# Third and fourth chain of an output projection's first pair change places; four small steps come later

## The chip, the cores and the metric

The kernel runs on one core of a Trainium2 chip. The metric is the device time of one execution in microseconds; 2374.19 is the median of the runs of the kernel before. Engines are named as in the profile: PE is TensorE's matmuls, PEld its weight loads, DVE is VectorE, ACT is ScalarE, POOL is GpSimd, SP is SyncE, whose queue starts the weight transfers.

## The reference

Two residual layers over 256 positions of width 2048 in float32, each followed by a SwiGLU feed-forward block; RMSNorm ahead of every part and once at the end.

```
for layer in range(2):
    h = rms_norm(x, mix_norm[layer])
    if layer == 0:   # Mamba-2 SSD heads and latent-attention (MLA) heads behind one input projection
        z, xbc, dt_raw, c_q, c_kv, k_rope = split(h @ w_in)
        y_ssd = ssd_mixer(z, xbc, dt_raw, ...)       # dt = softplus(dt_raw + dt_bias); decay = exp(cumsum(dt * a))
        y_mla = mla_mixer(c_q, c_kv, k_rope, ...)    # 16 heads, softmax, k_pe = rope(k_rope)
        mix = concat(y_ssd, y_mla) @ w_out_even      # 4096 x 2048
    else:            # stick-breaking attention: log_keep = -softplus(z), cumulative sums, exp
        mix = stick_breaking_mixer(h, w_qkv, w_out_odd)
    x = x + mix
    x = x + (silu(n @ w_gate) * (n @ w_up)) @ w_down   # n = rms_norm(x, ffn_norm[layer])
return rms_norm(x, final_norm)
```

## The kernel before, in words

**Words.** Every float32 product is done in three passes: an operand is parted into high words (a cast on ACT, L345) and low words (source minus high words on DVE, L351), and high x high, low x high and high x low are added up in PSUM. A weight tile is 512 rows by 512 columns. It comes by DMA into a slot `w`; its high words go into one of the slots `wh` (three, later four, in turn), its low words overwrite the raw tile in its own slot. The casts of the weights keep the order of the chains in which they are used, whose order on PE is fixed.

**Pairs.** `pair` multiplies an operand by a pair of column blocks in the manner of Strassen and Winograd: seven products of sums, M1 to M7, go into four PSUM banks. M1, M6 and M7 add into bank z, M5 and M3 into p3, M2 into p2, M4 into p4. The rest of the depth is done in plain chains c0 to c3. In this text a chain is one such product on PE: 8 matmuls with a tile's high words and then 4 with its low words (all L786). After M1, M5, M6 and M7 ACT copies the bank out of PSUM (L807); the next chain on that bank waits for the copy.

**Sums of weights.** Two slots `wsum` hold sums that DVE makes (L733): t1 = b12 - b11 is the source of M5, t2 = b22 - t1 that of M6, b12 becomes b22 - b12, the source of M7, and M4's source is b21 - t2. As there are two slots, M4's source is written into the slot of M5's, after the last product that reads it there; it reads t2, so it must be done before M6's low words overwrite t2.

**Order.** PE runs in the order in which the program is written. ACT, DVE, POOL and SP are ordered by a scheduler after priorities: `urgent` gives steps that free a bank an early one, weights have a count that rises by 100 a step (`wprio`), and `issue_after` puts a step behind another. Small steps run as tasks beside the chains: `yield n` lets a task rest for n ticks, and a chain gives two ticks (one after half its high words), a projection's group of 12 matmuls in the plain parts about two.

**Where the changed lines work.** `project_residual` runs two pairs; the first uses the order LATE, the second HALF. It runs three times: for the SSD heads at about 320 us, for the MLA heads at about 512 us and for stick-breaking at about 1585 us. `norm_operand` and `operand_block` take a finished residual block apart again: 4 transposes for each half of the positions (L356), products with the gains (L665), squares. `stick_weights` makes the stick-breaking weights of four heads: logarithms (L1133, ACT, with a table load), sums (L1134). `dt_and_krope` makes dt, the decay's sums (`adt`, L1291; matmuls L1295 and L1296; `edec`, L1303), a transpose of the sums (L1307) and the rotated k_pe (POOL, L1323, L1326). `cb` (L1385) multiplies the convolved B and C, which end in silus (L1371). `constant_tiles` fills a tile (L268) on which PE's first matmuls (L308, `rouse`) run while the first data come.

Of the kernel before, what the change touches and what calls it, by code (L numbers as in the profile page):

```python
# [47 lines left out]
class Trunk:  # L48
# [215 lines left out]
    def constant_tiles(self, rows_m, rows_a, rows_b):  # L264
        nc = self.nc
        c = lambda shape, name, dt=F32: self.cp.tile(shape, dt, name=name)
        idle = self.s2([256])
        nc.vector.memset(idle, 1.0)  # L268
        self.idle = idle.bitcast(BF16)
        self.rouse(5)  # L270
        self.ident = c([P, P], "ident")
        make_identity(nc, self.ident)
        warm = self.small([P, 1], "warm")
        nc.scalar.activation(warm, self.ident[:, 0:1], AF.Exp)
        self.ident_r = c([P, P], "ident_r", F32R)
        nc.gpsimd.dma_start(self.ident_r.bitcast(F32), self.ident)
        self.identb = c([P, P], "identb", BF16)
        make_identity(nc, self.identb)
        ones = self.s2([P])
        nc.gpsimd.memset(ones, 1.0)  # L280

        self.tri_u = c([P, P], "tri_u")
        nc.gpsimd.affine_select(self.tri_u, ones, [[1, P]], ALU.is_ge, 0.0, base=0, channel_multiplier=-1)
        tri_l = self.s2([P])
        nc.gpsimd.affine_select(tri_l, ones, [[-1, P]], ALU.is_ge, 0.0, base=0, channel_multiplier=1)
        self.tri_l, self.ones_r = c([P, P], "tri_l", F32R), c([P, P], "ones_r", F32R)
        nc.gpsimd.tensor_copy(self.tri_l, tri_l)
        nc.gpsimd.tensor_copy(self.ones_r, ones)
        self.ones = self.ones_r.bitcast(F32)
        zero = self.s2([P])  # L290
        nc.gpsimd.memset(zero, 0.0)

        self.cmask = c([P, P], "cmask", BF16)
        nc.gpsimd.affine_select(self.cmask, zero, [[-1, P]], ALU.is_ge, NEG, base=0, channel_multiplier=1)

        self.vm, self.va, self.vb = c([P, 32], "vm"), c([P, 56], "va"), c([P, 120], "vb")
        self.g_mix = (self.vm[:, 0:16], self.vm[:, 16:32])
        self.g_ffn = (self.va[:, 0:16], self.va[:, 16:32])
        self.g_ssd, self.g_q, self.g_kv = self.va[:, 32:48], self.va[:, 48:52], self.va[:, 52:56]
        self.conv_b = self.vb[:, 96:120]  # L300
        self.vectors(rows_m, self.vm)
        self.late_vectors = lambda: (self.vectors(rows_a, self.va), self.vectors(rows_b, self.vb))
# [288 lines left out]
    def norm_operand(self, st, j, g):  # L591

        def squares():
            for t in range(2):
                self.square_sum(self.xres[j][:, t], st["ssq"][:, t, j:j + 1])
        self.operand_block(st, j, lambda t, k: self.xwords[j][:, t, k * P:(k + 1) * P],
                           g[:, 4 * j:4 * j + 4], squares, 9)

    def norm_begin(self):
        return {"ssq": self.small([P, 2, 4], "ssq"), **self.operand()}  # L600
# [24 lines left out]
    def project_residual(self, st, view, scale=None, done=None, held=()):  # L625
# [12 lines left out]
        for n in (0, 2):  # L638
            self.pair(st, view(n), view(n + 1), add(n), add(n + 1), self.HALF if n else self.LATE,
                      lambda m: self.head if n and m in held else None)  # L640
# [7 lines left out]
    def operand(self):  # L648
        return {"xT": [], "A": {}, "S": [], "N": []}

    def operand_block(self, st, j, src, g, then=None, wait=1):


        nc = self.nc

        def gen():
            res = []
            for t in range(2):
                yield 2 if t == 0 else 1
                pt = self.tr([4, P])  # L660
                for k in range(4):
                    self.transpose(pt[:, k], src(t, k))
                r = self.s2([4, P])
                with self.urgent():
                    nc.vector.tensor_tensor(r, pt, g.unsqueeze(2).to_broadcast([P, 4, P]),  # L665
                                            op=ALU.mult)
                res.append(r)
            if then:
                then()
            yield wait  # L670
            self.operand_ready(st, j, res, 1)
        st["xT"].append((self.spawn(gen()), None))
# [71 lines left out]

    MORE = ("M1", "M5", "c2", "t1", "t2", "t4", "n0", "n2", "n4", "M3", "M6", "M2", "t3", "M4", "n1", "M7", "n3", "c3")

    LATE = ("M1", "M5", "M3", "M6", "M2", "M7", "M4", "c0", "c1", "c2", "c3")

    def pair(self, st, va, vb, left, right, order=HALF, after=lambda m: None, homes={}):

# [5 lines left out]
        nc = self.nc  # L756
# [8 lines left out]
        src = {"M1": b11, "M3": b22, "M7": b12}  # L765
# [24 lines left out]
        def add(b, x, w, keep=None):  # L790

            wh, wl, slot = w
            n = len(x)
            for k, (hi, lo) in enumerate(x):
                mm(b, hi, wh[:, k])
                mm(b, lo, wh[:, k])
                if k == 1 and n > 2:
                    self.tick()
            for k, (hi, lo) in enumerate(x):
                self.clock += 1  # L800
                slot.used(mm(b, hi, wl[:, k], stop=k == n - 1), self.clock)
            self.tick()
            todo[b] -= 1
            if keep:
                with self.urgent():
                    o = kept[keep] = homes[keep] if keep in homes else self.s2([512])
                    copied = nc.scalar.copy(o, ps[b]).ins  # L807
                    if keep == "M5":
                        self.kept = copied
            with self.urgent():  # L810
                for c, q, take, t in (("p2", "M1", left, 0), ("p4", "M7", left, 1), ("z", "M5", right, 1),
                                      ("p3", "M6", right, 0)):
                    if todo[c] == 0 and q in kept:
                        todo[c] = -1
                        take(t, ps[c], kept[q])
# [27 lines left out]
        for m in order:  # L843
# [14 lines left out]
            if m == "n0":  # L858
                first = self.wsplit(raw["c0"], 4, 4, mybir.DependencyClass.Sync)
# [31 lines left out]
            if m[0] == "c":  # L891
                k0 = 8 + int(m[1]) // 2 * 4
                x = [[self.operand_tile(st, k0 + k, t) for k in range(4)] for t in range(2)]
                for b in ("z", "p3") if int(m[1]) % 2 else ("p2", "p4"):
                    add(b, x[b in ("z", "p4")], w)
                continue
            add(bank[m], ops(m), w, m if m in keeps else None)

    def residual_back(self):
# [208 lines left out]
    def stick_weights(self, qk, res, half):  # L1108

        nc = self.nc  # L1110
        N = 3 * P
        yield 5
        for t, _ in qk:
            self.join(t)
        zs, es, parts = [], [], []
        for h in range(4):
            qT, kT = (r[h // 2][:, h % 2] for _, r in qk)
            pz = self.at([N])
            nc.tensor.matmul(pz[:, P:N], kT[:, 0:P], qT, start=True, stop=True)
            nc.tensor.matmul(pz[:, 0:P], kT[:, P:S], qT[:, P:S], start=True, stop=True)  # L1120
            z, e = self.spare[4 * half + h][:, :N], self.s2([N])
            nc.scalar.activation(z, pz, AF.Copy, scale=P ** -0.5)
            nc.gpsimd.affine_select(z[:, 0:S], z[:, 0:S], [[0, 2], [1, P]], ALU.is_gt, NEG, base=0,
                                    channel_multiplier=-1)
            nc.scalar.activation(e, z, AF.Abs)
            last = nc.scalar.activation(e, e, AF.Exp, scale=-1.0)
            zs.append(z)
            es.append(e)
            yield 1
        yield 4  # L1130
        for z, e in zip(zs, es):
            with self.tc.issue_after(last.ins), self.tc.issue_after(self.cast):
                nc.scalar.activation(e, e, AF.Ln, bias=1.0)  # L1133
            nc.vector.scalar_tensor_tensor(e, z, 0.0, e, op0=ALU.max, op1=ALU.add)  # L1134

        def parted(e):
            eh, el = self.s2([N], F32R), self.s2([N], F32R)
            with self.urgent():
                self.split(eh, el, e)
            return eh, el  # L1140
        yield 3
        for h in range(4 + 2):
            if h < 4:
                parts.append(parted(es[h]))
            if h >= 2:
                z, (eh, el) = zs[h - 2], parts[h - 2]
                pc = self.at([N])
                for m, e in enumerate((eh, el)):
                    nc.tensor.matmul(pc, self.tri_l, e, start=m == 0, stop=False)
                for m, e in enumerate((eh, el)):  # L1150
                    nc.tensor.matmul(pc[:, 2 * P:N], self.ones_r, e[:, 0:P], start=False, stop=m == 1)
                nc.vector.tensor_tensor(z, z, pc, op=ALU.subtract)
                nc.scalar.activation(z, z, AF.Exp)
                res.append(z)
            yield 2
# [83 lines left out]
    def dt_and_krope(self, rstd, xT):  # L1239
        nc, i = self.nc, self.i  # L1240
# [39 lines left out]
        for m in range(nterm - 2, -1, -1):  # L1280
# [9 lines left out]
        self.adt = self.small(sh, "adt", bufs=1)  # L1290
        nc.vector.scalar_tensor_tensor(self.adt, self.dt, -1.0, ea.unsqueeze(1).to_broadcast(sh),  # L1291
                                       op0=ALU.mult, op1=ALU.mult)
        yield 11
        pa = self.at([2, 2, 32])
        nc.tensor.matmul(pa[:, 0], self.tri_u, self.adt, start=True, stop=True)  # L1295
        nc.tensor.matmul(pa[:, 1], self.ones, self.adt, start=True, stop=True)  # L1296
# [15 lines left out]

        nc.vector.memset(self.kpeT, 0.0)
        kp = self.s2([2, 2, 64])
        for t in range(2):
            self.apply_rope(kp[:, t, 0:1], dk[:, t:t + 1, 32:96], t, 1)
# [276 lines left out]
```

## Time and profile before

| what | value |
|---|---|
| median of the runs (lowest to highest) | 2374.19 us (2373.77 to 2375.26) |
| the profiled execution's own time | 2374.79 us |
| its span, mean granted clock | 2373.1 us, 0.999 |
| busy: PE, PEld, DVE, ACT, POOL | 99%, 82%, 84%, 62%, 9% |
| DMA | 486.33 MB, mean 205 GB/s |
| largest group on PE: L786 with high words | 3896 matmuls, 985.5 us |
| DVE's low words of weights, L351 | 399 of 2244 ns, 892.1 us |
| ACT's high words of weights, L345 | 399 of 1874 ns, 744.0 us |
| sums of weights on DVE, L733 | 52 of 2004 ns and 35 of 2038 ns |

Rows of the timeline give the start in us from the span's begin, the length, engine, line and operation, output <- inputs, how many in a row, and in brackets how long the engine had been idle before and what released it. Matmuls of 512 columns start every 0.23 us when nothing holds them; a row's length has the last one's way through the array in it.

### The profile page before, as it was taken

The page shows a single profiled execution, that of the slowest core. Times are in us where ns is not written, and L with a number is a line of the kernel's source. Part 1 is how long each engine was busy: PE and PEld are TensorE (multiplying, and loading weights), DVE is VectorE, ACT ScalarE, POOL GpSimd, SP SyncE. Part 2 cuts the span into 40 slices and gives each one's busy share as a digit, 9 for nine tenths or more (in the row PEclk, how much of TensorE's full clock was granted, in tenths as well). Part 3 has the DMA queues.
Part 4 walks back from the last instruction along what each step waited for, and adds up shares of the span by engine and source line. Part 5 has one row for each costly group of instructions (what it writes and reads, how often), then busy time and mean ns, then how long its engine had stood idle before and what let it go on. Part 6 is the DMA issues. An engine that isn't in the chain of part 4 may idle for free.

```text
span 2373.1 us, 28173 instructions
## 1 busy us (share of the span) xinstructions
PE 2351.7 (99%) x11083; PEld 1954.9 (82%) x11083; DVE 1984.2 (84%) x1639; ACT 1460.9 (62%) x1478; POOL 207.2 (9%) x257
## 2 busy tenths in 40 slices
PE   9999999999999999999999999999999999999998
PEld 7888888988888888888888888888888888888886
DVE  6776587588998889989888889779997988999884
ACT  6655565566665655566655786776665665556663
POOL 1342001110000000000000010000000000000011
PEclk9999999999999999999999999999999999999999
DMA  7655556545666777777676655556666777777773
GB/s 267 199 195 177 193 190 187 138 142 191 225 205 212 222 215 218 223 220 220 219 237 212 202 178 176 173 176 235 228 212 209 217 227 220 218 214 227 216 254 108
DMA packets 271396, 486.33 MB, mean 205 GB/s; under 512 B 22236, under 2 KB 47456, under 8 KB 271264
## 3 DMA queue, kind: packets, MB, share of 16 engines
q1 hardware_dynamic: 255264, 446.20, 57.3%
q0 software_dynamic: 15232, 37.01, 6.4%
q8 instruction: 87, 1.43, 0.2%
q10 hardware_dynamic: 768, 1.33, 0.2%
q14 instruction: 45, 0.37, 0.0%
HBM read 459.24 MB, written 25.20 MB: 204 GB/s over the span
## 4 chain that ended last, share of the span: by engine, by line
PE 86%; issue 7%; DVE 3%; ACT 2%; DMA 1%; POOL 0%; SPq 0%; POOLq 0%; ACTq 0%; DVEq 0%
PE acc L786 49%; PE acc L456 10%; PE acc L459 10%; PE acc L458 10%; PE tr L356 1%; ACT wh L345 1%; PE acc L500 1%; DVE w L351 1%; DVE wsum L733 1%; PE at L1445 1%; PE acc L502 0%; DVE wsum L351 0%; DMA w<-in_w_in_dram 0%; PE at L1516 0%; PE at L1517 0%
## 5 line engine op out<-in xcount | busy, mean ns | idle before, releaser
L351 DVE TENSOR_TENSOR w<-w,wh 128x2048 fp32r<-128x2048 f32 (+2 forms) x399 | 892.1, 2244 | 188.5 <-ACT wh L345 176.2
L786 PE MATMUL acc<-wh,s 128*128 128x512 f32 x3896 | 985.5, 391 | 3.7 <-ACT s L807 3.6
L345 ACT CAST wh<-w 128x2048 fp32r<-128x2048 f32 (+2 forms) x399 | 744.0, 1874 | 335.3 <-PE acc L459 139.8
L786 PEld LDWEIGHTS acc<-wh,s 128*128 128x128 f32 x3896 | 725.3, 188 | 153.9 <-ACT s L807 5.2
L456 PE MATMUL acc<-wh,s 128*128 128x512 f32 (+1 forms) x1216 | 482.9, 397 | 0.0
L459 PE MATMUL acc<-wh,s 128*128 128x512 f32 (+1 forms) x1216 | 471.3, 388 | 0.0
L458 PE MATMUL acc<-w,s 128*128 128x512 f32 (+1 forms) x1152 | 445.8, 387 | 0.5 <-DVE w L351 0.5
L786 PE MATMUL acc<-w,s 128*128 128x512 f32 x1312 | 356.0, 390 | 0.5 <-DVE w L351 0.4
L786 PEld LDWEIGHTS acc<-w,s 128*128 128x128 f32 x1312 | 246.0, 188 | 53.2 <-DVE w L351 2.0
L459 PEld LDWEIGHTS acc<-wh,s 128*128 128x128 f32 x1216 | 228.5, 188 | 47.5
L456 PEld LDWEIGHTS acc<-wh,s 128*128 128x128 f32 x1216 | 228.7, 188 | 44.9 <-issue 1.7
L458 PEld LDWEIGHTS acc<-w,s 128*128 128x128 f32 x1152 | 216.9, 188 | 42.9 <-issue 1.4
L351 DVE TENSOR_TENSOR wsum<-wsum,wh 128x2048 fp32r<-128x2048 f32 (+1 forms) x101 | 217.9, 2158 | 9.5 <-ACT wh L345 9.5
L345 ACT CAST wh<-wsum 128x2048 fp32r<-128x2048 f32 (+1 forms) x101 | 182.8, 1810 | 52.5 <-PE acc L786 23.8
L948 POOL DMA_DIRECT2D saved<-s x64 | 55.9, 995 | 1107.5 <-ACT s L947 1106.4
L345 ACT CAST wh<-lent 128x2048 fp32r<-128x2048 f32 (+1 forms) x62 | 114.6, 1858 | 61.1 <-PE acc L459 24.2
L351 DVE TENSOR_TENSOR lent<-lent,wh 128x2048 fp32r<-128x2048 f32 (+1 forms) x62 | 137.1, 2216 | 11.2 <-ACT wh L345 10.7
L733 DVE TENSOR_TENSOR wsum<-w,wsum 128x2048 f32<-128x2048 f32 (+1 forms) x52 | 104.2, 2004 | 19.9 <-PE acc L786 17.9
L786 PE MATMUL acc<-wsum,s 128*128 128x512 f32 x380 | 104.6, 390 | 1.4 <-DVE wsum L351 1.4
L786 PEld LDWEIGHTS acc<-wsum,s 128*128 128x128 f32 x380 | 71.2, 188 | 17.2 <-DVE wsum L351 2.3
L807 ACT COPY s<-acc 128x512 f32<-128x512 f32 x88 | 51.5, 587 | 39.6 <-PE acc L786 39.6
L733 DVE TENSOR_TENSOR wsum<-w,w 128x2048 f32<-128x2048 f32 (+1 forms) x35 | 71.3, 2038 | 1.4 <-DMA w<-in_w_qkv_dram 1.4
(267 smaller groups left out, 1878.6 us busy)
## 6 DMA issues: line engine op xcount, KB each, us to landing
w<-in_w_down_dram SPq DMA_DIRECT2D x80, 1024.0 KB, 5.0
w<-in_w_gate_dram SPq DMA_DIRECT2D x76, 1024.0 KB, 5.1
w<-in_w_up_dram SPq DMA_DIRECT2D x76, 1024.0 KB, 5.2
w<-in_w_qkv_dram SPq DMA_DIRECT2D x48, 1024.0 KB, 5.0
w<-in_w_in_dram SPq DMA_DIRECT2D x47, 1024.0 KB, 5.1
w<-in_w_out_even_dram SPq DMA_DIRECT2D x32, 1024.0 KB, 4.9
saved<-s POOLq DMA_DIRECT2D x64, 256.0 KB, 7.3
w<-in_w_out_odd_dram SPq DMA_DIRECT2D x16, 1024.0 KB, 5.0
```

The source lines that it names most:

```text
L345: cast = nc.scalar.copy(hi, src).ins
L351: return nc.vector.tensor_tensor(lo, src, hi.bitcast(F32), op=ALU.subtract).ins
L356: self.nc.tensor.transpose(out.bitcast(F32R), src, self.ident_r)
L456: nc.tensor.matmul(ps[t], hi[:, ts], wh, start=k == 0, stop=False)
L458: slot.used(nc.tensor.matmul(ps[t], hi[:, ts], wl, start=False, stop=False), self.clock)
L459: nc.tensor.matmul(ps[t], lo[:, ts], wh, start=False, stop=k == nk - 1)
L500: nc.tensor.matmul(ps[:, h % 2], wh[:, hs], x, start=k == n == 0, stop=False)
L733: ins = self.nc.vector.tensor_tensor(half(o, so), half(p, sp), half(q, sq), op=ALU.subtract).ins
L786: m = nc.tensor.matmul(ps[b], x, y, start=b not in started, stop=stop, skip_group_check=True)
L807: copied = nc.scalar.copy(o, ps[b]).ins
L948: nc.gpsimd.dma_start(self.saved[n][:, t], s, accum_op=ALU.add)
L1445: nc.tensor.matmul(py[:, ds], rows[c, h // 4][:, h % 4], xdt[c][:, ds], start=True, stop=True)
```

## The change

Six places. The order LATE has M6 as the third chain and M3 as the fourth. The task of the dt product rests 13 ticks instead of 11. The residual transposes rest 3 ticks at first instead of 2 and the rest after them is 8 instead of 9. The logarithms are put behind the last L807 copy written. k_pe's tile is cleared behind the idle tile's filling.

```diff
@@ constant_tiles
         idle = self.s2([256])
-        nc.vector.memset(idle, 1.0)
+        self.idle_filled = nc.vector.memset(idle, 1.0).ins
@@ norm_operand
         self.operand_block(st, j, lambda t, k: self.xwords[j][:, t, k * P:(k + 1) * P],
-                           g[:, 4 * j:4 * j + 4], squares, 9)
+                           g[:, 4 * j:4 * j + 4], squares, 8, 3)
@@ operand_block
-    def operand_block(self, st, j, src, g, then=None, wait=1):
+    def operand_block(self, st, j, src, g, then=None, wait=1, first=2):
...
             for t in range(2):
-                yield 2 if t == 0 else 1
+                yield first if t == 0 else 1
@@ pair
-    LATE = ("M1", "M5", "M3", "M6", "M2", "M7", "M4", "c0", "c1", "c2", "c3")
+    LATE = ("M1", "M5", "M6", "M3", "M2", "M7", "M4", "c0", "c1", "c2", "c3")
...
                     copied = nc.scalar.copy(o, ps[b]).ins
+                    self.copied = copied
@@ stick_weights
-            with self.tc.issue_after(last.ins), self.tc.issue_after(self.cast):
+            with self.tc.issue_after(last.ins), self.tc.issue_after(self.cast), self.tc.issue_after(self.copied):
                 nc.scalar.activation(e, e, AF.Ln, bias=1.0)
@@ dt_and_krope
-        yield 11
+        yield 13
         pa = self.at([2, 2, 32])
...
-        nc.vector.memset(self.kpeT, 0.0)
+        with self.tc.issue_after(self.idle_filled):
+            nc.vector.memset(self.kpeT, 0.0)
```

In the changed file line numbers are higher by one from L808 and by up to two further on.

**Order in the SSD heads' output projection.** DVE, around the third chain, before and then after (`w6` holds M3's source, `wsum11` M6's, `wsum10` M5's and then M4's; a name with an odd number is the low words' view of the same slot):

```order
L351 TENSOR_TENSOR w6_73<-w6_74,wh2_67 128x2048 [waits Activation_49]
L733 TENSOR_TENSOR wsum10_82<-w7_76,wsum11_84 128x2048 [waits DMAHW3_49,DVE_49,PE_49]
L351 TENSOR_TENSOR wsum11_83<-wsum11_84,wh3_68 128x2048 [waits Activation_49]
L351 TENSOR_TENSOR w7_75<-w7_76,wh0_65 128x2048 [waits Activation_49]
L351 TENSOR_TENSOR w5_71<-w5_72,wh1_66 128x2048 [waits Activation_49]
```

```order
L351 TENSOR_TENSOR w6_73<-w6_74,wh3_68 128x2048 [waits Activation_49]
L733 TENSOR_TENSOR wsum10_82<-w7_76,wsum11_84 128x2048 [waits DMAHW3_49,DVE_49,PE_49]
L351 TENSOR_TENSOR wsum11_83<-wsum11_84,wh2_67 128x2048
L351 TENSOR_TENSOR w7_75<-w7_76,wh0_65 128x2048 [waits Activation_49]
L351 TENSOR_TENSOR w5_71<-w5_72,wh1_66 128x2048 [waits Activation_49]
```

The steps keep their places on DVE; M3's and M6's high words have exchanged their slots. ACT at the same place, before and after:

```order
206 L345 CAST wh2_67<-w6_74 128x2048
207 L345 CAST wh3_68<-wsum11_84 128x2048
208 L807 COPY s2_271_2576<-acc_267_2557 128x512
209 L807 COPY s2_272_2593<-acc_268_2558 128x512
210 L345 CAST wh0_65<-w7_76 128x2048
211 L345 CAST wh1_66<-w5_72 128x2048
```

```order
206 L345 CAST wh2_67<-wsum11_84 128x2048
207 L345 CAST wh3_68<-w6_74 128x2048
208 L807 COPY s2_271_2576<-acc_267_2557 128x512
209 L807 COPY s2_272_2593<-acc_268_2558 128x512
210 L345 CAST wh0_65<-w7_76 128x2048
211 L345 CAST wh1_66<-w5_72 128x2048
```

The cast of M6's source now stands ahead of that of M3's.

**Order in the MLA heads' output projection.** DVE ahead of M4's source (`w8` holds M3's source, `mx` the maxima of a head's scores; the L1523 of before is L1525 in the changed file), before and after:

```order
L351 TENSOR_TENSOR s2_400_3900<-at_474_4283,s2_399_3899 128x256 [waits Activation_49]
L351 TENSOR_TENSOR s2_458_4249<-s2_427_4093,s2_457_4248 128x512 [waits Activation_49]
L1523 TENSOR_REDUCE mx_478_4309<-at_477_4302 128x1 [waits PE_49]
L1523 TENSOR_REDUCE mx_478_4309<-at_477_4302 128x1
L1524 TENSOR_SCALAR mx_478_4309<-mx_478_4309 128x2 [waits DVE_49]
L351 TENSOR_TENSOR s2_467_4265<-s2_313_3271,s2_466_4264 128x512 [waits Activation_49]
L351 TENSOR_TENSOR s2_469_4269<-s2_428_4094,s2_468_4268 128x512 [waits Activation_49]
L733 TENSOR_TENSOR wsum10_82<-w4_70,wsum11_84 128x2048 [waits DMAHW3_49,PE_49]
```

```order
L351 TENSOR_TENSOR s2_400_3900<-at_474_4283,s2_399_3899 128x256 [waits Activation_49]
L351 TENSOR_TENSOR w8_77<-w8_78,wh1_66 128x2048 [waits Activation_49]
L1525 TENSOR_REDUCE mx_478_4309<-at_477_4302 128x1 [waits PE_49]
L1525 TENSOR_REDUCE mx_478_4309<-at_477_4302 128x1
L351 TENSOR_TENSOR s2_467_4265<-s2_313_3271,s2_466_4264 128x512 [waits Activation_49]
L1526 TENSOR_SCALAR mx_478_4309<-mx_478_4309 128x2 [waits DVE_49]
L351 TENSOR_TENSOR s2_469_4269<-s2_428_4094,s2_468_4268 128x512 [waits Activation_49]
L733 TENSOR_TENSOR wsum10_82<-w4_70,wsum11_84 128x2048 [waits DMAHW3_49,PE_49]
```

The subtraction of M3's source, which stood twelve rows further up, now stands five rows ahead of L733.

**Order behind the dt product.** ACT, before and after:

```order
60 L1371 ACT_TABLE_LOAD
61 L1371 ACTIVATE s2_95_743<-s2_95_743 128x512
62 L1303 ACT_TABLE_LOAD
63 L1303 ACTIVATE edec_100_812<-edec_100_812 128x64
64 L1371 ACT_TABLE_LOAD
65 L1371 ACTIVATE s2_97_764<-s2_97_764 128x512
66 L345 CAST wh1_66<-w5_72 128x2048
```

```order
60 L1373 ACT_TABLE_LOAD
61 L1373 ACTIVATE s2_95_743<-s2_95_743 128x512
62 L1304 ACT_TABLE_LOAD
63 L1304 ACTIVATE edec_100_827<-edec_100_827 128x64
64 L345 CAST wh1_66<-w5_72 128x2048
65 L1373 ACT_TABLE_LOAD
66 L1373 ACTIVATE s2_97_764<-s2_97_764 128x512
```

The weight cast has gone ahead of the second silu (`s2_97`) and its table load. The orders of POOL and SP are the same as before.

## The prediction

> **What bounds the kernel now.** I read the page first, then the list of what TensorE waits for, then the timeline around each edit, one engine at a time.
>
> ```profile
> PE 2351.7 (99%) x11083; PEld 1954.9 (82%) x11083; DVE 1984.2 (84%) x1639; ACT 1460.9 (62%) x1478; POOL 207.2 (9%) x257
> ...
> PE 86%; issue 7%; DVE 3%; ACT 2%; DMA 1%; POOL 0%; SPq 0%; POOLq 0%; ACTq 0%; DVEq 0%
> ...
> PE acc L786 <- ACT s L807: 3.6, 4, 1.2
> ...
> PE at L1295 <- DVE adt L1291: 1.3, 1, 1.3
> ```
>
> PE is busy 99% of the span and holds 86% of the chain that ends last. The matmuls neither grow nor shrink in number, so an edit counts only by what it adds to or takes from PE's waits. In the two rows of waits (engine, line, what it waits for; us in all, times, longest) they are few: the longest after the start are 1.2 and 1.3 us. The kernel can gain no more here than the waits that an edit meets, and it loses whatever new wait stands in PE's queue, which runs in the order written.
>
> **Third and fourth chain, output projection of the SSD heads.** These are the three engines in turn, columns start, length, engine, line, operation:
>
> ```profile
> 324.42 1.07 PE L786 MATMUL acc<-wsum,s 128*128 128x512 f32 x4
> 326.17 2.11 PE L786 MATMUL acc<-wh,s 128*128 128x512 f32 x8 [0.68 <-ACT s L807]
> ...
> 332.51 1.98 PE L786 MATMUL acc<-wh,s 128*128 128x512 f32 x8
> 334.32 1.07 PE L786 MATMUL acc<-w,s 128*128 128x512 f32 x4
> ...
> 342.88 1.21 PE L786 MATMUL acc<-w,s 128*128 128x512 f32 x4 [0.20 <-DVE w L351]
> ...
> 320.74 1.90 ACT L345 CAST wh<-w 128x2048 fp32r<-128x2048 f32 x1
> 322.53 1.92 ACT L345 CAST wh<-wsum 128x2048 fp32r<-128x2048 f32 x1
> ...
> 322.67 2.33 DVE L351 TENSOR_TENSOR w<-w,wh 128x2048 fp32r<-128x2048 f32 x1 [2.99 <-ACT wh L345]
> 325.53 2.29 DVE L733 TENSOR_TENSOR wsum<-w,wsum 128x2048 f32<-128x2048 f32 x1 [0.53 <-PE acc L786]
> 327.74 2.28 DVE L351 TENSOR_TENSOR wsum<-wsum,wh 128x2048 fp32r<-128x2048 f32 x1
> ```
>
> One chain is 8 matmuls of the high words and 4 of the low, 332.51 to 334.32 to about 335.23: 1.81 + 0.91 = 2.72 us. M5 ends near 325.4. The third chain, M3, writes M5's bank and so waits for M5's copy: 0.68, and with the slower start of the weights 0.84 over the pace. M6 writes M1's bank, whose copy is done by then; that wait goes.
>
> But M6's low words stand behind two DVE steps. L733 makes M4's source from M6's, into M5's slot, so it can't begin before M5's last product (the row at 325.53 waits for PE). Only then may the subtraction at 327.74 overwrite M6's source. Before, that pair ended at 329.94, and M3's 2.72 us of matmuls covered it, as M6's low words came at 331.6. Now nothing stands between. The order on ACT gives M6's cast first (320.74 to 322.5) and M3's second (to 324.4); on DVE M3's subtraction still stands ahead of L733. So DVE begins M3's at 324.5 instead of 322.67, ends at 326.7, does L733 to 328.95 and M6's low words to 331.2. PE does M6's high words from 325.3 to 327.15 and stands still for 4.05 us. M3 then needs 2.72 and the four-by-four transposes twice (0.29 each): the fourth chain ends at 331.2 + 0.91 + 3.3 = 335.4, where it ended at 332.51. That is +2.9. The wait at 342.88 (with its slow start 0.47) comes after DVE work that no longer is late: it goes. **+2.4**; the ends are +1.1, if L733 could run as soon as M5 ends (325.5 + 4.4 = 329.9, 1.3 sooner) and the later wait goes as well, and +3.0, if that wait stays.
>
> **The same in the output projections of the MLA heads and of stick-breaking.**
>
> ```profile
> 521.77 1.20 PE L786 MATMUL acc<-wh,s 128*128 128x512 f32 x4 [1.22 <-ACT s L807]
> ...
> 525.63 0.38 PE L1516 MATMUL at<-s,s 128*128 128x128 f32 x2
> ...
> 509.52 2.29 DVE L351 TENSOR_TENSOR w<-w,wh 128x2048 fp32r<-128x2048 f32 x1 [1.13 <-ACT wh L345]
> 520.74 2.28 DVE L733 TENSOR_TENSOR wsum<-w,wsum 128x2048 f32<-128x2048 f32 x1
> 523.02 2.27 DVE L351 TENSOR_TENSOR wsum<-wsum,wh 128x2048 fp32r<-128x2048 f32 x1
> ...
> 1591.52 2.11 PE L786 MATMUL acc<-wh,s 128*128 128x512 f32 x8 [0.68 <-ACT s L807]
> ...
> 1597.10 0.59 PE L1074 MATMUL at<-spare,s 128*128 128x256 f32 x2
> ...
> 1590.88 2.29 DVE L733 TENSOR_TENSOR wsum<-w,wsum 128x2048 f32<-128x2048 f32 x1 [5.13 <-PE acc L786]
> 1593.09 2.28 DVE L351 TENSOR_TENSOR wsum<-wsum,wh 128x2048 fp32r<-128x2048 f32 x1
> ```
>
> MLA: the order moves M3's subtraction (2.29, at 509.52) to just ahead of the last maxima before L733; the softmax ahead of it, no longer behind those 2.29, runs some 1.7 earlier on ACT and pays most of it back. Following the new order with these lengths I get L733 from 521.5 and M6's low words ready at 526.05 (525.3 before). M6, with its 0.91 of low matmuls, ends at 527.0; the third chain ended at 525.63. **+1.4**, from +0.3 (low words ready as before, M6 hidden behind the copies) to +3.0 (the 2.29 not paid back at all). The copy wait of 1.22 is inside this count.
>
> Stick: DVE is idle 5.13 before L733, so nothing else interferes. L733 and low words end at 1595.35; PE does M6's high words from 1590.7 (1591.52 less the 0.84 of that wait) to 1592.5 and waits 2.85. M6 ends at 1596.3, M3 at 1599.0, against 1597.10: **+1.9**, from +1.2, if the waits that follow in the next group take some of it back, to +2.0.
>
> **The dt product.** Its two small matmuls come two steps (12 matmuls of 0.23, 2.7 us) later.
>
> ```profile
> 76.75 0.41 PE L1295 MATMUL at<-adt,tri_u 128*128 128x64 f32 x2 [1.28 <-DVE adt L1291]
> ...
> 85.89 1.05 PE L1385 MATMUL at<-s,s 128*128 128x128 f32 x8
> ...
> 81.62 1.28 ACT L1371 ACT_TABLE_LOAD   x1 [0.19 <-DVE s L1369]
> 82.91 0.64 ACT L1371 ACTIVATE s<-s 128x512 f32<-128x512 f32 x1
> 83.45 1.89 ACT L345 CAST wh<-w 128x2048 fp32r<-128x2048 f32 x1
> ```
>
> The wait of 1.28 (1.45 over the pace) goes. But ACT's order now has the weight cast ahead of the second table load and silu: cast from 81.43, where ACT now falls idle (81.62 less 0.19), to 83.3, table to 84.6, silu to 85.25. PE, 1.45 earlier, reaches the first L1385 at about 84.3; its third matmul reads that silu and waits some 0.65. **-0.8**, from -1.4 (the cast waits for its slot and the silu slips ahead in time) to 0 (the cast late, and with it the silu by its whole 1.89). The transposes L1307 and L1323 cost PE the same, later; POOL's rope and the DMA of the decay rows hang on L1307, 2.7 us later, and are needed a whole projection later: nothing.
>
> **Residual transposes** (two per normalised block) come one half chain later.
>
> ```profile
> 570.44 1.28 DVE L617 TENSOR_TENSOR xres<-s,xres 128x512 f32<-128x512 f32 x2
> ...
> 571.82 0.51 PE L356 MATMUL tr<-ident_r,xwords 128*128 128x128 f32 x4 [0.89 <-PE tr L356]
> ...
> 629.24 1.20 PE L786 MATMUL acc<-wsum,s 128*128 128x512 f32 x4 [0.70 <-DVE wsum L351]
> ...
> 557.70:617.00 59.30, 59.26 (x52) 1.00 0.68 228
> ```
>
> The second set waits until the residual sums of 570.44 end (571.7). Half a chain later it doesn't: 1.07 over the pace at 571.82, of which 0.95 goes. But the last row, DVE's busy time in that window, is 59.26 of 59.30, so PE ahead of it meets it again; the wait at 629.24 may grow by a third of that. **-0.6**, from -0.95 to -0.2. In stick and at the other blocks PE waits for nothing there: 0.
>
> **Logarithms after the copy**, two groups of stick-breaking.
>
> ```profile
> 1512.86 2.11 PE L786 MATMUL acc<-wh,s 128*128 128x512 f32 x8 [0.99 <-ACT s L807]
> ...
> 1510.10 1.28 ACT L1133 ACT_TABLE_LOAD   x1
> ...
> 1512.24 0.56 ACT L807 COPY s<-acc 128x512 f32<-128x512 f32 x1
> ...
> 1513.94 5.52 ACT L345 CAST wh<-w 128x2048 fp32r<-128x2048 f32 x3
> ```
>
> The copy goes ahead of the table load and two of the logarithms: M7 starts 1.15 sooner. The casts behind them all stay at 1513.94, since ACT does the same work before: PE waits for the next weights (1.9 for the cast: 1515.85) as long as it did in two places before. 0; the later subtraction behind the logarithms costs some 0.1 in each of two groups: **+0.2**, from -1.1 (the casts come sooner) to +0.5.
>
> **k_pe's clearing** lies ahead of the idle tile's filling, on which PE's first matmuls wait:
>
> ```profile
> 0.98 0.48 DVE L1315 MEMSET kpeT<- 128x512 f32 x1 [0.98 <-PEq L1584]
> ...
> 7.44 1.09 PE L358 MATMUL tr<-ident,xres 128*128 128x128 f32 x4 [1.56 <-DMA xres<-in_x_dram]
> ...
> 9.18 0.63 PE L458 MATMUL acc<-w,s 128*128 128x512 f32 x1
> 9.60 0.63 PE L459 MATMUL acc<-wh,s 128*128 128x512 f32 x1
> ```
>
> PE may start 0.48 sooner, but at 7.44 it waits 1.56 for x from DRAM, which covers it: 0, at best -0.5 if the clock rises that much sooner.
>
> **The sum**: 2.4 + 1.4 + 1.9 - 0.8 - 0.6 + 0.2 + 0 = +4.5, on the profiled execution's 2374.79 (span 2373.1 and 1.7 around it) 2379.3. That execution lies 0.6 above the median of the runs, 2374.19, from which the forecast is **2378.7**. What a measurement of this kernel can tell from no change is about 0.2%, 4.75 us: faster is below 2369.4, slower above 2378.9. My sum lies just inside.
>
> **Rivals.** *The clock falls in the long wait: slower.* The matmuls at 9.18 and 9.60 are 0.42 apart, against 0.23 later; the chip runs PE at half pace after its idle start, from 1.80 until about 10. A wait of 4.05 us, three times the longest so far, could bring that back at 327 to 331. From the wait at 7.44 the slow stretch lasts to 10.0, 2.6 us; from the start, 8.2 us: half of that is lost, 1.3 to 4.1 us. It decides where the wait outlasts whatever the clock's watch needs; after waits of up to 1.3 us the matmuls go on at 0.23 to 0.26 (2.11 for eight at 326.17), and no row after the start has a longer wait. At 2.5 the time is 2381.2. [...] The waits of this trace are too short to say.
>
> *The delays are absorbed: no change.* PE comes later at all waits behind the three places; of these 571.82 and 629.24 (1.07 + 0.86 over the pace) are DVE's. If DVE isn't late with PE, MLA's 1.4 is gone by 630, and with SSD at its lower end the time is 2374.2 + 1.1 + 0 + 1.9 - 0.8 + 0.2 = 2376.6. Against it: ahead of 557.7 DVE itself waits for casts, and those for PE.
>
> *The swap pays: faster.* If M6's low words were ready with its high words, the copy waits 0.84 + 1.38 + 0.84 go, with dt 1.45, the transposes 0.95 and the second wait at 342.88 0.47: -5.9, 2368.3. It needs L733 ahead of M5's end; the row at 325.53, which waits for PE, is against it in all three places.
>
> **How the numbers follow.** The sum's case 0.65, its terms' ends giving about +2 to +6.5, half of it on each side of 2378.9; absorbed 0.15; clock 0.10; swap pays 0.10, of which 0.06 below 2369.4. Faster 0.06; same 0.33 + 0.15 + 0.04 = 0.52; slower 0.32 + 0.10 = 0.42. The range 2374.5 to 2382.0 leaves out the paying swap (0.10), half of the clock case (0.05) and a few hundredths of the sum's own ends.
>
> **What would show it.** In the profile of the changed kernel: a wait of L786 on "DVE wsum L351" of about 4 us near 327 to 331, and of near 2.9 at 1592 (less 2), and no L807 wait at the three places; no wait at L1295, one of about 0.6 at L1385; none at the L356 of 572; at 1512 the wait on L807 exchanged for one on a cast or DVE. It is wrong if M6's low words come before PE asks for them, if later waits shrink by what these add, or if PE's clock drops.

## The result: 0.35% slower, and the profile after

The changed kernel took 2382.95 us in the median (2380.93 to 2383.60, 6 runs) against 2374.10 (2373.77 to 2375.26, 6 runs): a ratio of 1.0035, 95% interval 1.0024 to 1.0046, or +8.85 us. The forecast was 2378.7, within 2374.5 to 2382.0. The profiled execution took 2381.85, its span is 2380.1 and its mean granted clock 0.997 instead of 0.999.

What TensorE waits for, in the list of waits of the changed kernel (engine and line, what it waits for; us in all, times, longest):

```profile
PE acc L786 <- DVE wsum L351: 9.0, 5, 3.9
PE tr L358 <- DMA xres<-in_x_dram: 1.6, 1, 1.6
PE acc L786 <- ACT s L807: 1.5, 1, 1.5
PE acc L786 <- ACT wh L345: 1.3, 1, 1.3
```

The waits for the copy L807 have fallen from 3.6 us to 1.5, and those for low words of a sum have grown from 1.4 to 9.0. The SSD heads' projection in the timeline, PE, then ACT, then DVE, and behind them PE's busy time, granted clock (0.77) and DMA share in the stretch from 325 to 340:

```profile
324.18 1.97 PE L786 MATMUL acc<-wh,s 128*128 128x512 f32 x8
330.08 2.07 PE L786 MATMUL acc<-wsum,s 128*128 128x512 f32 x4 [3.92 <-DVE wsum L351]
331.95 0.67 PE L356 MATMUL tr<-ident_r,twinwords 128*128 128x128 f32 x4
332.42 2.04 PE L786 MATMUL acc<-wh,s 128*128 128x512 f32 x4
...
334.72 1.61 PE L786 MATMUL acc<-wh,s 128*128 128x512 f32 x4
336.16 1.09 PE L786 MATMUL acc<-w,s 128*128 128x512 f32 x4
...
319.59 1.91 ACT L345 CAST wh<-wsum 128x2048 fp32r<-128x2048 f32 x1
321.39 1.91 ACT L345 CAST wh<-w 128x2048 fp32r<-128x2048 f32 x1
...
323.33 2.29 DVE L351 TENSOR_TENSOR w<-w,wh 128x2048 fp32r<-128x2048 f32 x1 [4.80 <-ACT wh L345]
325.54 2.28 DVE L733 TENSOR_TENSOR wsum<-w,wsum 128x2048 f32<-128x2048 f32 x1
327.74 2.29 DVE L351 TENSOR_TENSOR wsum<-wsum,wh 128x2048 fp32r<-128x2048 f32 x1
...
325.00:340.00 15.00, 11.07 (x43) 8.61 (x42) 14.15 (x9) 9.48 (x8) 0.00 (x0) 0.77 0.17 58
```

The three DVE rows stand end to end, M3's subtraction, M4's source, M6's low words, and PE waits for the third. Then four matmuls of M6 take 2.07 us where four take 1.07 to 1.09, and the next four 2.04: they start 0.43 apart, not 0.23. The pace is the old one again after the third matmul of the row at 334.72, which starts at 335.69. From 330.08 to that start it is 5.61 us; where the clock held (e5 below) the same matmuls and transposes need 3.16. The slow stretch costs 2.5 us.

The other places, PE (dt product, MLA's third chain, residual transposes, logarithms, stick-breaking's third chain):

```profile
84.82 0.71 PE L1387 MATMUL at<-s,s 128*128 128x128 f32 x4 [0.63 <-ACT s L1373]
...
526.07 1.21 PE L786 MATMUL acc<-wh,s 128*128 128x512 f32 x4 [1.51 <-ACT s L807]
...
530.07 1.20 PE L786 MATMUL acc<-wsum,s 128*128 128x512 f32 x4 [0.89 <-DVE wsum L351]
...
576.83 0.96 PE L356 MATMUL tr<-ident_r,xwords 128*128 128x128 f32 x8
...
1520.71 2.14 PE L786 MATMUL acc<-wh,s 128*128 128x512 f32 x8 [1.28 <-ACT wh L345]
...
1600.35 1.20 PE L786 MATMUL acc<-wsum,s 128*128 128x512 f32 x4 [2.77 <-DVE wsum L351]
```

Setting the start of each matmul against that of the same matmul before, the difference of the two profiled executions grows or shrinks here: at the start -0.5 us, dt product -0.7 (together -1.2 at 88), SSD projection +5.2 (+4.0 at 344), MLA projection +1.5 (+5.5 at 560), residual transposes -0.9 at 572 and +0.3 back at 622, where eight matmuls take 2.37 instead of 2.00 (+4.9 at 640), then -0.3 spread evenly up to 1300 without a wait, logarithms +0.3 (+4.9 at 1580), stick-breaking's projection +2.1, and 0.1 behind it; in all +7.1. The median of the runs lies another 1.1 above this execution. That part does not stand in this trace; the experiments trace it to the clock.

### The profile page after: what moved, and what is told of

It reads as the page before. It is cut to its first block, busy times and chain, and to the rows that moved or that the text cites. A ratio compares the mean times of both kernels' runs of the same rounds, so it can differ in the third digit from the quotient of the medians.

```text
span 2380.1 us, 28173 instructions
## 1 busy us (share of the span) xinstructions
PE 2354.1 (99%) x11083; PEld 1957.3 (82%) x11083; DVE 1984.9 (83%) x1639; ACT 1461.3 (61%) x1478; POOL 206.7 (9%) x257
## 4 chain that ended last, share of the span: by engine, by line
PE 86%; issue 7%; DVE 3%; ACT 3%; DMA 0%; POOL 0%; SPq 0%; POOLq 0%; ACTq 0%; DVEq 0%
PE acc L786 49%; PE acc L456 11%; PE acc L459 10%; PE acc L458 10%; PE tr L356 1%; ACT wh L345 1%; PE acc L500 1%; DVE wsum L733 1%; DVE w L351 1%; DVE wsum L351 1%; PE at L1447 1%; PE acc L502 0%; PE at L1518 0%; PE at L1519 0%; POOL spare L1124 0%
## 5 line engine op out<-in xcount | busy, mean ns | idle before, releaser
L733 DVE TENSOR_TENSOR wsum<-w,wsum 128x2048 f32<-128x2048 f32 (+1 forms) x52 | 104.2, 2004 | 14.8 <-PE acc L786 12.8
L807 ACT COPY s<-acc 128x512 f32<-128x512 f32 x88 | 51.5, 587 | 42.2 <-PE acc L786 42.2
L733 DVE TENSOR_TENSOR wsum<-w,w 128x2048 f32<-128x2048 f32 (+1 forms) x35 | 71.4, 2039 | 3.8 <-DMA w<-in_w_out_even_dram 1.9
```

The lines of the kernel that those rows point to most:

```text
L733: ins = self.nc.vector.tensor_tensor(half(o, so), half(p, sp), half(q, sq), op=ALU.subtract).ins
```

## The experiments

**The old order alone put back (e1).** Edit to the changed kernel:

```diff
-    LATE = ("M1", "M5", "M6", "M3", "M2", "M7", "M4", "c0", "c1", "c2", "c3")
+    LATE = ("M1", "M5", "M3", "M6", "M2", "M7", "M4", "c0", "c1", "c2", "c3")
```

> The changed kernel with the old order of the third and fourth chain; the other five edits stay. Theory: the exchange carries the whole loss, and the other five edits are a small gain as the two traces show them (start -0.5, dt -0.7, transposes -0.3, logarithms +0.1): about 2372.7 us, 1.4 under the kernel before, granted clock back at 0.999. Rival: the other edits carry part of the loss, for instance by work moved into the stretch of the SSD heads' projection: 2374.5 us or more.

2372.96 us (2372.18 to 2373.78, 11 runs) against 2374.03 for the kernel before, run beside it, ratio 0.9995 (0.9986 to 1.0004), granted clock 0.999. The exchange carries the whole loss. The other five edits are worth about -1.1 by the medians, which the interval does not part from nothing.

**The exchange alone (e2).** The edit of the change to LATE, in the kernel before.

> The kernel before with the exchange of the third and fourth chain alone. Theory: its price is what the traces show at the three places, +5.2 (of it 2.5 from the clock), +0.9 and +2.3, and some 1 more by the medians: 2382.5 to 2384.5 us, granted clock 0.997. Rival, that the loss needs the other edits as well: 2379 us or less.

2383.82 us (2383.68 to 2384.11, 5 runs), ratio 1.0041 (1.0028 to 1.0055), clock 0.997, as the theory had it in all; of its parts the MLA projection is +1.5, not +0.9, in this trace too. The trace shows the same fall of the clock at 330, and a second one in stick-breaking's projection. PE there, and the windows' row of that place with a granted clock of 0.89:

```profile
1600.81 1.25 PE L786 MATMUL acc<-wsum,s 128*128 128x512 f32 x4 [2.77 <-DVE wsum L351]
1601.86 3.56 PE L786 MATMUL acc<-wh,s 128*128 128x512 f32 x8
1605.26 1.09 PE L786 MATMUL acc<-w,s 128*128 128x512 f32 x4
...
1595.00:1610.00 15.00, 12.23 (x49) 9.72 (x48) 14.09 (x9) 9.57 (x9) 0.00 (x0) 0.89 0.34 116
```

Eight matmuls of M3 take 3.56 instead of 1.98: 1.6 us lost, after a wait of only 2.77. In the trace of the changed kernel the same wait, 2.77 at 1600.35, was not followed by a slow stretch. So the second fall comes in some executions only.

**PE kept at work in the first wait (e3).** In the changed kernel, ahead of the low words of M6 in the SSD heads' projection, matmuls whose result nothing reads:

```diff
+            if keep == "M6" and self.fill:     # 16 in the first pair of the SSD heads' projection, else 0
+                self.rouse(self.fill)
             for k, (hi, lo) in enumerate(x):
                 self.clock += 1
```

> The changed kernel with 16 idle matmuls (512 columns, result unused) between the high and the low words of M6 in the SSD heads' projection, so that PE works through 3.5 of the 4.1 us in which it waits; the wait's end, set by DVE, stays. Theory: the clock fell because PE stood idle, so the matmuls after 330 go at 0.23 and the time drops by the 2.5 us of the slow stretch or a little more: 2379.5 to 2380.5 us, runs closer together. Rival: the slow stretch comes from something else, such as weights or banks that come late behind DVE: the pace after 330 stays at 0.43 and the time at 2383.

2381.13 us (2379.86 to 2383.34, 6 runs), ratio 1.0030 (1.0018 to 1.0042). PE in the first place, then in the MLA heads' projection, then in stick-breaking's, and the windows' row of the MLA heads' with a granted clock of 0.91:

```profile
325.90 3.63 PE L309 MATMUL tr<-s 128*128 128x512 bf16 x15
329.83 1.19 PE L789 MATMUL acc<-wsum,s 128*128 128x512 f32 x4 [0.30 <-DVE wsum L352]
...
331.15 1.16 PE L789 MATMUL acc<-wh,s 128*128 128x512 f32 x4
...
523.59 1.58 PE L789 MATMUL acc<-wh,s 128*128 128x512 f32 x4 [1.80 <-ACT s L812]
...
1598.67 1.49 PE L789 MATMUL acc<-wsum,s 128*128 128x512 f32 x4 [2.77 <-DVE wsum L352]
1599.95 3.32 PE L789 MATMUL acc<-wh,s 128*128 128x512 f32 x8
...
510.00:530.00 20.00, 18.20 (x84) 15.01 (x84) 15.95 (x25) 15.08 (x28) 0.00 (x0) 0.91 0.31 109
```

In the first place the wait's end stays with DVE, and the matmuls behind it run at full pace (four in 1.19 and 1.16 us, the granted clock 1.00 from 325 to 340): the fall there came from PE standing idle. But the time is above what was expected and the runs lie as far apart as before. In this execution the clock fell in two other places: in stick-breaking's projection, and in the MLA heads' after a wait for the copy of 1.80, where four matmuls take 1.58 and the slow stretch costs some 0.7 net, as the wait for low words that follows in the changed kernel (0.89) is gone. The theory of one place did not do.

**Both waits covered (e5), and both in part (e6).** The same hook, with matmuls of 256 columns on a constant: 32 in the SSD heads' projection and 20 in stick-breaking's; then 12 and 8.

```diff
+                out = self.tr([512])
+                for _ in range(2 * self.fill):   # fill 16 and 10, then 6 and 4
+                    nc.tensor.matmul(out[:, 0:256], self.identb, self.ident.bitcast(BF16), start=True, stop=True)
```

> The changed kernel with idle matmuls (256 columns, result unused) between the high and the low words of M6 in two places: 32 in the SSD heads' projection (3.5 of 4.1 us of waiting) and 20 in stick-breaking's (2.2 of 2.9 us). The traces of the runs so far show the clock falling in the second place too, in some executions. Theory: with both covered it falls nowhere, the granted clock is 0.999 and the time is the waits alone, 2374.1 + 4.6 = 2378.7 us, with the runs within 1.5 us. Rival: the clock still falls in one of the places, or in a third: 2380 us or more and runs far apart.

> The same with fewer of them, 12 and 8 (1.3 and 0.9 us), so that PE idles 2.7 us in the SSD heads' projection and 2.0 us in stick-breaking's. [...] If 2.7 us are enough in some executions, as stick-breaking's 2.8 us seem to be, some runs lie 1.5 to 2.5 us higher, with a granted clock of 0.998 or 0.997.

Both covered: 2379.13 us (2378.80 to 2379.78, 11 runs), ratio 1.0020 (1.0011 to 1.0030), clock 0.999 in all runs. The slowest of them is faster than all 6 runs of the changed kernel (2380.93 at least). This is the price of the waits alone: 4.9 us over 2374.24, the kernel before, run beside it. The MLA heads' projection was not covered here, and the clock held there too, after a wait for the copy of 1.5. Covered in part: 2381.76 us (2380.17 to 2383.50, 6 runs), ratio 1.0031 (1.0020 to 1.0043), with clocks from 0.999 to 0.997. PE at the two waits of the partly covered kernel, and between them in the MLA heads' projection:

```profile
330.25 1.19 PE L789 MATMUL acc<-wsum,s 128*128 128x512 f32 x4 [2.60 <-DVE wsum L352]
...
524.73 1.20 PE L789 MATMUL acc<-wh,s 128*128 128x512 f32 x4 [1.99 <-ACT s L814]
...
1599.43 1.19 PE L789 MATMUL acc<-wsum,s 128*128 128x512 f32 x4 [1.89 <-DVE wsum L352]
```

In this execution the clock held at all three. It took 2381.02 even so, some 1.4 above that of the full cover, 1.0 of it by the end of the MLA heads' projection; so a longer time alone does not show a fall. The granted clocks of the other runs, 0.998 in three and 0.997 in one, point to falls, the 0.998 weakly, as 2 of the 28 runs of the kernel before read it too. Where the clock fell in them no trace shows. With the idle time cut to about half a microsecond in both places (0.42 and 0.57 in e5's trace) it never fell, in 11 runs.

**The cause of the wait taken away (e4).** M4's source gets a slot of the transfers instead of the slot of M5's source:

```diff
-                src["M4"] = self.wsum()
+                src["M4"] = self.wtile() if order is self.LATE else self.wsum()
```

> The changed kernel with M4's source made in a slot of the transfers (w) in these pairs, not in that of M5's source, so that the sum need not wait for M5's last product and M6's low words are ready with its high words. Theory: the three waits (4.1, 2.7 with the copy, 2.9) and the fall of the clock go, and with them the copy waits of the kernel before: about 2371.5 us. Rival: a weight transfer behind it finds one slot less and comes late, or DVE's new order makes another low part late: part of it comes back, 2374 to 2378 us.

2370.60 us (2369.58 to 2371.90, 11 runs), ratio 0.9985 (0.9977 to 0.9994), clock 0.999: 12 us under the changed kernel, and 3.4 under the kernel before. DVE at the place, and then PE at stick-breaking's residual transposes:

```profile
320.83 2.33 DVE L351 TENSOR_TENSOR wsum<-wsum,wh 128x2048 fp32r<-128x2048 f32 x1 [1.46 <-ACT wh L345]
...
1631.88 0.51 PE L356 MATMUL tr<-ident_r,xwords 128*128 128x128 f32 x4 [1.38 <-issue]
```

M6's low words are made at 320.83, long before PE asks; they now also stand ahead of M3's subtraction on DVE (323.08), which came first in the changed kernel. So the waits for the copy and for low words are both gone at all three places. Of the gain 1.5 us comes back at 1631.88, where PE, now earlier, waits for a residual sum on DVE.

**The slot with the old order (e7).** The edits of e1 and e4 together.

> M4's source in a transfer slot, as in the kernel that came out at 2370.6, but with the old order of the third and fourth chain. Theory: the exchange is worth something only where M6's low words are ready; with the old order the copy waits (0.84, 1.4, 0.84) come back, so 2372.5 to 2373.5 us, about the 2372.96 of the old order without that slot. Rival: the gain came from the slot alone, by M4's and later sums coming sooner: 2370.6 us as well.

2373.12 us (2371.92 to 2374.69, 11 runs), ratio 0.9995 (0.9987 to 1.0004). The copy waits are back (2.0 us in three places in its list of waits), and the time is that of e1. So, each against its own kernel before, the exchange is worth 2.3 us (-3.4 with it, -1.1 without) where the slot is there, and no run of e4 is as slow as the fastest of e7 (2371.90 against 2371.92); without the slot it costs some 10 (+8.85 with it, -1.1 without).

**Later transposes on top (e8).** To e4, for stick-breaking's blocks only:

```diff
-                           g[:, 4 * j:4 * j + 4], squares, 8, 3)
+                           g[:, 4 * j:4 * j + 4], squares, *((7, 4) if g is self.g_ffn[1] else (8, 3)))
```

> M4's source in a transfer slot and the new order, and in stick-breaking the residual transposes another half chain later, where the trace shows a new wait of 1.56 us over the pace for the residual sums at 1632. Theory: that wait goes or shrinks to 0.2, 2369.3 us. Rival: DVE is the limit there, and the wait comes back at the next low words (1689): 2370.6 us.

2370.44 us (2369.35 to 2373.00, 11 runs), ratio 0.9985 (0.9976 to 0.9994): the same as e4. The wait at 1632 is gone, and PE waits later:

```profile
1677.15 1.88 PE L786 MATMUL acc<-wh,s 128*128 128x512 f32 x7 [1.01 <-DVE s L380]
```

DVE is busy 59.90 of the 60 us from 1620 to 1680: it is the limit in this stretch, as the rival had it, though the wait came back at 1677 and not at 1689.

## Why the prediction was wrong

- **The waits: right, and to size.** Predicted 4.05 and 2.85 us for M6's low words, measured 3.92 and 2.77. Of the 3.92 some 1.2 is M3's subtraction, an estimate: M5's last product ended near 324.3, and L733 began behind that subtraction, at 325.54; the rest is the slot. Of the places, the SSD heads' was put at +2.4 and is +2.7 without the slow stretch, the MLA heads' at +1.4 and is +1.5, stick-breaking's at +1.9 and is +2.1. In the MLA heads' projection 0.3 of it is a longer wait for the copy (1.51), which stands behind a softmax step on ACT. The sum with all other edits was put at +4.5; with the clock held up it is +4.9 (e5), and 2379.13 is what 2378.7 forecast.
- **The clock: the step that failed.** It was a rival with a chance of 0.10 and a price of 2.5. The price was right for the place, 2.5 in the trace, by luck in part, as it was taken from a span of 1.3 to 4.1. The chance was not: all six runs of the changed kernel and all five of e2 have a clock of 0.997. The trace of before has no wait above 1.3 us after the start, so it could not say which wait brings the clock down, and I let that silence stand for a small chance. The 0.10 was my estimate; no run shows where such a chance would come from. What the runs show in its place: a wait of 3.92 brought the clock down in both traces that have it, and the 0.997 of all eleven runs agrees; one of 2.77 brought it down in e2 and e3 and not in the changed kernel's trace, and one of 1.80 did in e3. And I put the question to the longest wait only, so the second place, 1.6 us in e2, was in no sum. The two together, 4.1, make the +4.0 between e5 (+4.9) and the changed kernel (+8.85).
- **The range.** It took the clock as another case beside the sum, up to 2382.0, half of that case left out. A rival that adds to the likeliest case, at the very place that the case itself predicts, belongs in the range whole: 2378.7 + 2.5 + 1.6 = 2382.8.
- **dt product:** the new wait for the second silu, 0.65 predicted, is 0.63; -0.7 against -0.8. **Residual transposes:** the wait at 572 is gone, -0.9 against -0.95, and 0.3 came back as foreseen, at 622 and not at the wait of 629; -0.6 in all, as predicted. **Logarithms:** +0.3 against +0.2, the copy's wait exchanged for one on a cast (1.28 at 1520.71), as told.
- **Start:** 0 predicted, -0.5 here and -1.0 in e1's trace at matmul 54. This is not shown to be the edit: e2, which leaves k_pe's clearing where it was, has -1.1 there, and e7, which has the edit, -0.2. PE's first matmul does come 0.54 sooner in every trace with the edit, but behind it PE waits for x from DRAM, as the prediction said, and that wait differs from trace to trace (1.6 us in all before and in the changed kernel, 1.3 in e7).
- **The delays are absorbed** and **the swap pays** were rightly thought unlikely; what the second needs, the sum for M4 ahead of M5's end, is what e4 gave it.

## What to carry to other kernels

Before two steps change places, look for what their *sources* share: here the waiting was not for the bank that the exchange set free, but for a slot that made one sum wait for another product. A stall of TensorE is to be priced twice, once as the wait and once as the slow matmuls that may follow: here 3.92 us of idling cost another 2.5, 2.77 another 1.6 (e2), 1.80 some 0.7 net (e3). Where the stall couldn't be removed, matmuls without use kept the pace: with 32 and 20 of them the granted clock was 0.999 in all 11 runs (e5), 3.8 us under the changed kernel. When a rival's trigger is something that the forecast itself predicts, it is not an alternative but a further term of the sum.

## What the runs showed of the hardware

TensorE's pace fell to 0.43 us for a 512-column matmul, from 0.23, after an idle stretch of 3.92 us (SSD heads' projection, at once at 330.08, until 335.69) and, in some executions, of 2.77 us (stick-breaking's, in e2 from 1601.86 to 1605.26). In the second place the four matmuls right behind the wait, at 1600.81, still ran nearly at full pace (1.25 us for the four), and the slow ones came a microsecond later.

The granted clock reads the same. In the windows' rows of the changed kernel, with PE's busy time behind the length and the granted clock third from the end, it is 0.50 for the 6.82 us around the slow stretch of the first wait, 1.00 ahead of it and behind it, and 1.00 at the wait of 2.77 in stick-breaking's projection:

```profile
325.00:328.86 3.86, 1.15 (x6) 0.61 (x4) 3.86 (x3) 3.56 (x2) 0.00 (x0) 1.00 0.31 119
328.87:335.69 6.82, 5.61 (x18) 4.44 (x19) 6.34 (x5) 3.03 (x4) 0.00 (x0) 0.50 0.00 0
335.71:340.00 4.29, 4.29 (x20) 3.54 (x19) 3.94 (x2) 2.86 (x3) 0.00 (x0) 1.00 0.32 96
...
1598.00:1606.00 8.00, 5.65 (x27) 4.80 (x28) 8.00 (x5) 6.41 (x7) 0.00 (x0) 1.00 0.05 7
```

The waits of these traces, side by side: 3.92 was followed by slow matmuls in the changed kernel and in e2; 2.77 was in e2 and e3 (0.89 over 15 us in both) and was not in the changed kernel; 1.80 was in e3 (0.91 over 20 us); 2.60, 1.99 and 1.89 were not in e6, nor 1.51 in the changed kernel. So the length of a wait did not decide it alone; what else does is not shown here. In the SSD heads' projection 3.63 and 3.67 us of matmuls without use left 0.30 (e3) and 0.42 us (e5) of the wait, and the pace held behind both.

At the start of the program the matmuls run at the slow pace too (0.42 and 0.43 us apart at 9.18, 9.60 and 10.03 in the kernel before), but the granted clock reads 1.00 in that window. The trace of the kernel before holds no reading of the clock ahead of 10.16 us, so that 1.00 says nothing, and the pace of the matmuls is the sign there. This row of the kernel before (2 to 10 us) has it behind the busy times of the five engines; after the waits it read 0.77 and 0.89:

```profile
2.00:10.00 8.00, 6.44 (x19) 3.67 (x18) 2.32 (x6) 4.18 (x9) 5.75 (x11) 1.00 0.97 322
```
